# A hybrid attention/retention/MoE block: expert weights in 2 MB blocks of 16 KB runs, keys padded with zeros to 128 rows, second expert product 512 columns wide

## The chip, the cores and the metric

The kernel runs on one core of one Trainium2 chip. The metric is the device time of one execution in microseconds (us), taken as the median of several runs. A profile of one execution shows where that time goes. All times here are those of the kernel before the change.

## The reference, cut to what matters

The input is 512 tokens of width 1024, everything in float32.

```
xn   = rms_norm(h)
proj = xn @ w_in                      # 9728 columns: attention q/k/v, retention q/k/v/gate, branch gates
A: for each of 3 groups of 8 heads (head width 64): rotary on q and k, then
   scores = q . k / 8 in a window (groups 1 and 2: tokens strided by 4), masked softmax, times v
B: retention in both directions, chunks of 128, group norm, swish gate
h  = h + (sig(gA) * (A @ W_A) + sig(gB) * (B @ W_B)) @ w_out
hn = rms_norm(h)
router: top-1 of 8 expert groups, top-2 of 8 experts inside it (64 experts in all)
expert(x) = (silu(x @ w1[e]) * (x @ w3[e])) @ w2[e]     # w1, w3: 1024 x 512, w2: 512 x 1024
h  = h + weighted sum of the two experts of each token; final rms_norm
```

The weights of the 64 experts are 3 x 64 x 1024 x 512 x 4 bytes = 402.65 MB, and every one of them is read once.

## The kernel before, in words

There are two parts. In the first, the token-wise mixer, TensorE does long runs of products with `w_in`, the branch weights and `w_out`. Each weight tile and each activation is split into a high and a low half (`wH`, `wL`, `xH`, `xL`), and three products of 512 columns (L267 to L269 or L273 to L275) make one float32 product. A projection (`project`) of 512 columns has 8 x 4 x 3 such products. The program's order on each engine comes from a scheduler; it lays the products of one projection between the small products of the attention that came before.

Attention: `rotary_to` copies a projection to `qT` or `kT` (heads lie in pairs: block b holds head 2b on partitions 0 to 63 and head 2b+1 on partitions 64 to 127), exchanges halves by DMA into `sw`, multiplies on VectorE (L314) and GpSimd (L315) and adds on GpSimd (L316). The scores of a head are a product with 64 rows of `qT` against 64 rows of `kT`: L595 in `windows` (group 0, 192 keys per head, for two of the four token blocks in two parts of 64 queries), L639 (groups 1 and 2, 128 keys per head). A float32 product is two instructions on TensorE. VectorE masks them and finds the maximum (L551), ScalarE does the exponential (L553), TensorE transposes (L557), and the products with v follow (L604, L607, L648). There are 4 token blocks x 8 heads for each group.

In the second part, the experts go in 16 groups of 4. For a group, the tokens are gathered by products with a one-hot matrix (L769) into `xT` (32 slots per expert), then 16 blocks of `w13` (L973) and 8 blocks of `w2` (L1026, each 128 output columns of the four experts) are used. Between them stand the silu and the product of the halves (L993, L994), four transposes (L997) and copies (L999, L1000). The result is split (L1009, L1010) and scattered back (L1017 to L1019). The four experts of a group sit in four 32-column strips of TensorE's array.

Every block is 1 MB, 128 partitions x 8 KB, loaded by one DMA from SyncE's queue (`load`, L936) in program order. `wtile` hands out the places: eleven in `wA`; then two halves of `big`, used once; then a ring of the eleven and five more, four that hold the halves of the merged activation until `w_out` has read them (`xH0`, `xL0`, `xH1`, `xL1`) and one (`wB`) that lies where the mixer's weight halves were. The eleven and `big` lie where the mixer's right-hand pools were, which close after the last branch product. The loads of the first two weight tiles of a projection and of `w_out` (`raw`, L103) go on the same SyncE queue.

The last group of experts takes its `w2` in pieces of 256, 256, 256, 128 and 128 columns, each split, scattered and squared at once (`finish`), then the final norm and the output follow.

Of the kernel before, what the change touches and what calls it, by code (L numbers as in the profile page):

```python
# [10 lines left out]
F32 = mybir.dt.float32  # L11
# [10 lines left out]
P = 128  # L22
# [15 lines left out]
NWA = 11  # L38
NK2 = 4
# [29 lines left out]
def hybrid_block(ctx, tc, a, out):  # L69
# [86 lines left out]
    class Halves:  # L156


        def __init__(self):
            self.t = []  # L160
            for i in range(2):
                t_ = xp.tile([P, 4, S], F32R, name=self.tag + "01"[i])
                self.t.append(t_)
# [7 lines left out]
    class Hi(Halves):  # L171
        tag = "xH"

    class Lo(Halves):
        tag = "xL"
# [11 lines left out]
    xH = Hi()  # L187
    xL = Lo()
# [106 lines left out]
    def rotary_to(dst, dilated):  # L295
# [4 lines left out]
        def evac(b, ps):  # L300
# [8 lines left out]
            for k in range(2):  # L309
# [6 lines left out]
                nc.gpsimd.tensor_tensor(d, d, w, op=ALU.add)  # L316
# [228 lines left out]
    rec0 = at.tile([P, NT, REC], F32, name="rec0")  # L545
    orders = (nat, dil4, dil4)
# [15 lines left out]
    def windows(qT, kT, v4):  # L562
# [14 lines left out]
        for t in range(NT):  # L577
# [9 lines left out]
            for slot, hh in enumerate((0, 1, 4, 5)):  # L587
                po = (hh % 2) * HD
                ps = tmp()
                sm = rp.tile([P, 512], F32, name="sd", bufs=6)  # L590
                for i in range(2):
                    cs = slice(i * W, (i + 1) * W)
                    blk = hh // 2 + i
                    for qs, k0 in parts_:
                        nc.tensor.matmul(ps[qs, cs], qT[po:po + HD, blk, t * P + qs.start:t * P + qs.stop],  # L595
                                         kT[po:po + HD, blk, k0:k0 + W], start=True, stop=True)
                    probs(rec, hh + 2 * i, ps[:, cs], sm[:, cs], masks[:, mo_:mo_ + W])
                prT = transposed_probs(ps, sm, 3)
                oc = slice(slot * (HD + 1), (slot + 1) * (HD + 1))
                for i in range(2):  # L600
                    full = slice(2 * i * P, (2 * i + 1) * P)
                    po = i * HD
                    for qs, k0 in parts_:
                        nc.tensor.matmul(po_ps[i][qs, oc], prT[:, full][:, qs],  # L604
                                         values(k0 + po, 0, P, hh + 2 * i), start=True, stop=False)
                    for qs, k0 in parts_:
                        nc.tensor.matmul(po_ps[i][qs, oc], prT[po:po + HD, P:2 * P][:, qs],  # L607
                                         values(k0 + (1 - i) * P, po, HD, hh + 2 * i), start=False, stop=True)
            for i in range(2):
                nc.scalar.copy(rec[:, :NH * (HD + 1)].rearrange("p (x z w) -> p x z w", x=2, z=2)[:, :, i],  # L610
                               po_ps[i][:, :4 * (HD + 1)].rearrange("p (x w) -> p x w", x=2))

    for g in range(3):
        qT, kT = qk_tiles()
        project_in(512 * g, None, rotary_to(qT, g > 0))
        project_in(1536 + 512 * g, None, rotary_to(kT, g > 0))
# [8 lines left out]
        if g == 0:  # L625
            windows(qT, kT, v4)
            continue
        for t in range(NT):
            rec_t = at.tile([P, REC], F32, name="rec", bufs=2)
            rec = rec_t[:, :]  # L630
            for h0 in range(0, NH, 4):
                ps = tmp()
                sm = rp.tile([P, 512], F32, name="sd", bufs=6)
                for i in range(4):
                    hh = h0 + i
                    po = (hh % 2) * HD
                    cs = slice(i * P, (i + 1) * P)
                    ts = slice(t * P, (t + 1) * P)
# [86 lines left out]
    yrH = Hi()  # L725
    yrL = Lo()
# [12 lines left out]
    mH = Hi()  # L739
    mL = Lo()  # L740
# [23 lines left out]
    wA = ctx.enter_context(tc.tile_pool(name="wA", bufs=NWA, side="right"))  # L764

# [148 lines left out]
    w2 = a["moe_w2c"]  # L914
    nw = [0]
    spare = [(xp, "xH0"), (xp, "xL0"), (xp, "xH1"), (xp, "xL1"), (mo, "wB")]
    big0 = big.tile([P, 2 * 2048], F32, name="big")
    res = [None]

    def wtile():  # L920
        i = nw[0]
        nw[0] += 1
        if NWA <= i < NWA + 2:
            return big0[:, (i - NWA) * 2048:(i - NWA + 1) * 2048]
        i = (i if i < NWA else i - 2) % (NWA + len(spare))
        if i < NWA:
            t_ = wA.tile([P, 2048], F32, name="wa")
        else:
            pool, tag = spare[i - NWA]
            t_ = pool.tile([P, 2048], F32, name=tag)  # L930
# [12 lines left out]
    def experts(g, ranks, cols=None, first=False):  # L943
# [7 lines left out]
        xT = mo.tile([P, NK, P], F32, name="xT", bufs=3)  # L951
# [37 lines left out]
        ohT = mo.tile([P, S], F32R, name="k2", bufs=NK2)  # L989
        nc.scalar.copy(ohT, ps)  # L990

        sl = mo.tile([P, FF], F32, name="k2", bufs=NK2)
# [5 lines left out]
        hdT = mo.tile([P, 4, P], F32, name="k2", bufs=NK2)  # L998
# [5 lines left out]
        yH = mo.tile([P, D], F32R, name="xT", bufs=3)  # L1004
        yL = mo.tile([P, D], F32R, name="xT", bufs=3)
# [159 lines left out]
```

## Time and profile before

| | |
|---|---|
| median of 3 runs (lowest, highest) | 1665.96 us (1661.69, 1669.53) |
| the profiled execution: time, span from first to last instruction | 1663.84 us, 1662.1 us |
| TensorE, VectorE, ScalarE, GpSimd busy | 83%, 34%, 20%, 11% of the span |
| mean granted TensorE clock | 0.913 of full speed |
| DMA | 476.56 MB, mean 287 GB/s |

Busy shares are means over parts with different limits, so they have to be read part by part: the profile cuts the span into 40 slices, and a stretch of it can be asked for by its start and end.

### The profile page before, as it was taken

The numbers are of one execution on the slowest core, as the hardware profiler recorded it, in microseconds if no ns is written. First come the engines' busy times: TensorE is split into PE (matmuls) and PEld (weight loads), VectorE is DVE, ScalarE is ACT, GpSimd is POOL, SyncE is SP. The second block draws the span as 40 slices with busy tenths as digits, with TensorE's granted clock in tenths as the row PEclk, the third lists the DMA queues.
The fourth block names the chain that finished last, engine by engine and source line by source line (L and its number), as shares of the span: only waits on it lengthen the run. The fifth ranks groups of instructions, "written<-read, shape, count | busy, mean of one in ns | idle before, by whom it ended". The sixth has DMA issues, their size and how long they took to land. (4 is left out here: it accounts for less than half of the span.)

```text
span 1662.1 us, 27242 instructions
## 1 busy us (share of the span) xinstructions
PE 1386.6 (83%) x11699; PEld 915.9 (55%) x11699; DVE 561.7 (34%) x1241; ACT 328.7 (20%) x618; POOL 182.4 (11%) x137
## 2 busy tenths in 40 slices
PE   7999999999999999988776776776776786687674
PEld 6878787686876778754442442342353354244243
DVE  7556463554634544442220120120221121022014
ACT  5332334334346333210000000000000000000002
POOL 2214260231502211000000000000000000000001
PEclk9999999999999999998987887897898788888787
DMA  6324343233323423989999999999999999999995
GB/s 179 111 77 105 91 137 90 77 102 96 96 90 90 141 76 107 398 341 421 421 421 422 422 422 422 422 421 422 422 421 421 422 422 422 421 422 421 422 421 213
DMA packets 98509, 476.56 MB, mean 287 GB/s; under 512 B 17296, under 2 KB 17808, under 8 KB 49168
## 3 DMA queue, kind: packets, MB, share of 16 engines
q1 hardware_dynamic: 97344, 474.76, 72.8%
q8 instruction: 94, 1.54, 0.4%
q14 instruction: 31, 0.25, 0.0%
q10 hardware_dynamic: 1040, 0.00, 0.0%
HBM read 459.96 MB, written 4.26 MB: 279 GB/s over the span
## 5 line engine op out<-in xcount | busy, mean ns | idle before, releaser
L973 PE MATMUL acc<-wa,xT 128*32 128x512 f32 x1408 | 212.4, 716 | 83.7 <-DMA wa<-in_moe_w_dram 83.7
L213 DVE SCALAR_TENSOR_TENSOR wL<-raw,nwx,wH 128x512 fp32r<-128x512 f32 x152 | 138.0, 937 | 106.8 <-ACT wH L212 106.6
L268 PE MATMUL acc<-xL,wH 128*128 128x512 f32 x416 | 172.0, 413 | 0.0
L267 PE MATMUL acc<-xH,wH 128*128 128x512 f32 x416 | 168.8, 406 | 1.2 <-ACT kT L667 1.2
L973 PEld LDWEIGHTS acc<-wa,xT 128*32 128x32 f32 x1408 | 37.7, 117 | 237.2 <-DMA wa<-in_moe_w_dram 176.2
L269 PE MATMUL acc<-xH,wL 128*128 128x512 f32 x416 | 168.0, 404 | 0.0
L1026 PE MATMUL acc<-wa,k 128*32 128x128 f32 x2816 | 113.9, 319 | 56.8 <-DMA wa<-in_moe_w2c_dram 52.4
L1026 PEld LDWEIGHTS acc<-wa,k 128*32 128x32 f32 x2816 | 89.0, 129 | 81.2 <-DMA wa<-in_moe_w2c_dram 65.0
L212 ACT ACTIVATE wH<-raw,nwx 128x512 fp32r<-128x512 f32 x152 | 103.1, 716 | 150.1 <-PE acc L275 55.8
L273 PE MATMUL acc<-wH,xH 128*128 128x512 f32 x320 | 127.6, 400 | 0.2 <-ACT rt L536 0.2
L274 PE MATMUL acc<-wL,xH 128*128 128x512 f32 x320 | 127.5, 398 | 0.1
L275 PE MATMUL acc<-wH,xL 128*128 128x512 f32 x320 | 127.4, 398 | 0.0
L994 DVE SCALAR_TENSOR_TENSOR k<-k,gsl,acc 128x512 f32<-128x512 f32 x16 | 12.0, 748 | 332.8 <-issue 283.2
L769 PE MATMUL tmp<-oh,h 128*128 128x128 f32 x960 | 110.6, 276 | 0.3 <-DVE big L1019 0.3
L769 PEld LDWEIGHTS tmp<-oh,h 128*128 128x128 f32 x960 | 108.7, 192 | 3.7 <-DVE big L1019 3.2
L152 POOL TENSOR_TENSOR rr<-rv,mhalf 128x1 f32<-128x1 f32 x8 | 4.9, 622 | 947.0 <-ACT jk L1061 935.9
L1010 DVE TENSOR_TENSOR xT<-acc,xT 128x512 fp32r<-128x512 f32 (+2 forms) x35 | 22.6, 646 | 231.9 <-ACT xT L1009 231.8
L267 PEld LDWEIGHTS acc<-xH,wH 128*128 128x128 f32 x416 | 78.4, 189 | 22.4 <-issue 2.5
L268 PEld LDWEIGHTS acc<-xL,wH 128*128 128x128 f32 x416 | 78.5, 189 | 21.5 <-issue 2.3
L269 PEld LDWEIGHTS acc<-xH,wL 128*128 128x128 f32 x416 | 78.5, 189 | 18.1 <-issue 1.5
L1019 DVE TENSOR_TENSOR big<-big,tmp 128x512 f32<-128x512 f32 (+2 forms) x132 | 76.6, 635 | 21.7 <-PE tmp L1018 21.7
L1017 PE MATMUL tmp<-xT,k 128*128 128x512 f32 (+2 forms) x140 | 61.5, 462 | 22.9 <-ACT xT L1009 22.1
(259 smaller groups left out, 1705.3 us busy)
## 6 DMA issues: line engine op xcount, KB each, us to landing
wa<-in_moe_w_dram SPq DMA_DIRECT2D x176, 1024.0 KB, 19.8
wa<-in_moe_w2c_dram SPq DMA_DIRECT2D x88, 1024.0 KB, 19.9
raw<-in_w_in_dram SPq DMA_DIRECT2D x76, 512.0 KB, 3.7
xH<-in_moe_w_dram SPq DMA_DIRECT2D x32, 1024.0 KB, 19.8
xL<-in_moe_w_dram SPq DMA_DIRECT2D x31, 1024.0 KB, 19.7
xL<-in_moe_w2c_dram SPq DMA_DIRECT2D x16, 1024.0 KB, 19.8
xH<-in_moe_w2c_dram SPq DMA_DIRECT2D x16, 1024.0 KB, 19.8
wB<-in_moe_w_dram SPq DMA_DIRECT2D x15, 1024.0 KB, 19.6
```

Of the source, the lines that this page charges most:

```text
L212: nc.scalar.activation(wH[:, k, :], raw[:, k, :], AF.Copy, scale=sc)
L213: nc.vector.scalar_tensor_tensor(wL[:, k, :], raw[:, k, :], sc, wH[:, k, :], op0=ALU.mult, op1=ALU.subtract)
L267: nc.tensor.matmul(ps[tt], wh[:, cs], srcH.blk(kt), **fl)
L268: nc.tensor.matmul(ps[tt], wh[:, cs], srcL.blk(kt), start=False, stop=False)
L269: nc.tensor.matmul(ps[tt], wl[:, cs], srcH.blk(kt), start=False, stop=(kt == nk - 1))
L273: nc.tensor.matmul(ps[tt], aH, wh, **fl)
L274: nc.tensor.matmul(ps[tt], aH, wl, start=False, stop=False)
L275: nc.tensor.matmul(ps[tt], aL, wh, start=False, stop=(kt == nk - 1))
L769: nc.tensor.matmul(gp[j // 4][:, (j % 4) * P:(j % 4 + 1) * P], h[:, t, j * P:(j + 1) * P], oh_t.rearrange("p e c -> p (e c)"), start=(t == ...
L973: nc.tensor.matmul(p_[e * CAP:(e + 1) * CAP, :], xT[:, j, e * CAP:(e + 1) * CAP], wt[:, e * FF:(e + 1) * FF], start=(j == 0), stop=(j == N ...
L1019: nc.vector.tensor_tensor(hs_[:, t, cs], (h if first else hs_)[:, t, cs], ps, op=ALU.add)
L1026: nc.tensor.matmul(py[e * CAP:(e + 1) * CAP, o:o + P], hdT[:, i, e * CAP:(e + 1) * CAP], w4[:, e, i, :], start=(i == 0), stop=(i == 3))
```

## The change

The blocks of expert weights become 2 MB, 128 partitions x 16 KB: one for each of the eight 128-row slices of `w13` holds w1 and w3 of the four experts; one for each of the four 128-row slices of `w2` holds all 1024 output columns. The high and low halves of an activation move into one tile of 16 KB a partition for each half of the width (`x0`, `x1`), so that each of them is one place for a block. The places are five `wA`, `big` and `wk` (each used once), `x0`, `x1` and two `wB`: eleven in all, of which nine form the ring. The work tiles of a group lie where `wk` was. The `w2` products of all but the last group write 512 columns and end both halves of the output at the last block. The last group keeps blocks of output columns, and its last block comes in two DMAs.

The keys are written by GpSimd into `kP`, with a copy for the even and one for the odd head of a block, in which the other head's 64 partitions are zero. One product over 128 rows then gives the scores of both heads of a block side by side: 384 columns in group 0, 256 in groups 1 and 2. The added sum becomes two adds of 64 partitions, and two memsets zero `kP` once. `kP` has one buffer where `kT` had two.

```diff
-NWA = 11
+NGRP = NE // EG
+NWA = 5
+NWB = 2
+SLOT = 4096
...
+    def hi_lo():
+        t = []
+        for i in range(2):
+            t_ = xp.tile([P, 2, 4, S], F32R, name=f"x{i}")
+            t.append(t_)
+        return [Part([t_[:, z] for t_ in t]) for z in range(2)]
...
-                nc.gpsimd.tensor_tensor(d, d, w, op=ALU.add)
+                if pad is None:
+                    nc.gpsimd.tensor_tensor(d, d, w, op=ALU.add)
+                else:
+                    for z in range(2):
+                        hp = slice(z * HD, (z + 1) * HD)
+                        nc.gpsimd.tensor_tensor(pad[hp, b - 1 + k, z, :], d[hp], w[hp], op=ALU.add)
...
+    kP = at.tile([P, 4, 2, S], F32, name="kP")
+    for z in range(2):
+        nc.gpsimd.memset(kP[(1 - z) * HD:(2 - z) * HD, :, z, :], 0.0)
...
-            for slot, hh in enumerate((0, 1, 4, 5)):
+            for slot in range(4):
...
+                for qs, k0 in parts_:
+                    nc.tensor.matmul(ps[qs, :2 * W], qT[:, slot, t * P + qs.start:t * P + qs.stop],
+                                     kP[:, slot, :, k0:k0 + W], start=True, stop=True)
                 for i in range(2):
-                    for qs, k0 in parts_:
-                        nc.tensor.matmul(ps[qs, cs], qT[po:po + HD, blk, t * P + qs.start:t * P + qs.stop],
-                                         kT[po:po + HD, blk, k0:k0 + W], start=True, stop=True)
-                    probs(rec, hh + 2 * i, ps[:, cs], sm[:, cs], masks[:, mo_:mo_ + W])
+                    probs(rec, hh + i, ps[:, cs], sm[:, cs], masks[:, mo_:mo_ + W])
...
+                for i in range(0, 4, 2):
+                    nc.tensor.matmul(ps[:, i * P:(i + 2) * P], qT[:, (h0 + i) // 2, ts], kP[:, (h0 + i) // 2, :, ts],
+                                     start=True, stop=True)
                 for i in range(4):
-                    nc.tensor.matmul(ps[:, cs], qT[po:po + HD, hh // 2, ts], kT[po:po + HD, hh // 2, ts],
-                                     start=True, stop=True)
-                    probs(rec, hh, ps[:, cs], sm[:, cs], masks[:, 3 * HD:3 * HD + P] if g == 1 else masks[:, 9 * HD:])
+                    probs(rec, h0 + i, ps[:, cs], sm[:, cs],
+                          masks[:, 3 * HD:3 * HD + P] if g == 1 else masks[:, 9 * HD:])
...
+    ring = [(wA, "wa")] * NWA + [(xp, "x0"), (xp, "x1")] + [(mo, "wB")] * NWB
+    once = [(big, "big"), (wk, "wk")]
+    slots = ring[:NWA] + once + ring[NWA:]
...
+        pool, tag = slots[i] if i < len(slots) else ring[(i - len(slots)) % len(ring)]
+        t_ = pool.tile([P, SLOT], F32, name=tag, bufs={"wa": NWA, "wB": NWB}.get(tag, 1))
...
         for j in range(NK):
+            wt = load(block(w13, g, j)).rearrange("p (w e f) -> p w e f", w=2, e=EG)
             for w_, p_ in enumerate((p1, p3)):
-                wt = load(block(w13, g, 2 * j + w_))
                 for e in range(EG):
                     nc.tensor.matmul(p_[e * CAP:(e + 1) * CAP, :], xT[:, j, e * CAP:(e + 1) * CAP],
-                                     wt[:, e * FF:(e + 1) * FF], start=(j == 0), stop=(j == NK - 1))
+                                     wt[:, w_, e, :], start=(j == 0), stop=(j == NK - 1))
...
         if cols is None:
+            py = [acc(), acc()]
+            for i in range(4):
+                wt = load(block(w2r, g, i)).rearrange("p (e d) -> p e d", e=EG)
+                for hf in range(2):
+                    for e in range(EG):
+                        nc.tensor.matmul(py[hf][e * CAP:(e + 1) * CAP, :], hdT[:, i, e * CAP:(e + 1) * CAP],
+                                         wt[:, e, hf * 512:(hf + 1) * 512], start=(i == 0), stop=(i == 3))
             css = [slice(0, 512), slice(512, D)]
-            for cs in css:
-                py = acc()
-                for b in range(4):
-                    columns(load(block(w2, g, cs.start // P + b)), py, b * P)
-                split(cs, py, nc.scalar)
+            for cs, p_ in zip(css, py):
+                split(cs, p_, nc.scalar)
             scatter(css)
...
-    nc = _bacc.Bacc("TRN2", target_bir_lowering=False, num_devices=1)
+    nc = _bacc.Bacc("TRN2", target_bir_lowering=False, num_devices=1, dynamic_dma_scratch_size=1024)
```

## Rows read from the trace of the kernel before

**Rows 1.** The page's second part, the span in 40 slices of 41.6 us: the busy share of TensorE in tenths, and what the DMA engines moved.

```profile
PE   7999999999999999988776776776776786687674
...
GB/s 179 111 77 105 91 137 90 77 102 96 96 90 90 141 76 107 398 341 421 421 421 422 422 422 422 422 421 422 422 421 421 422 422 422 421 422 421 422 421 213
```

**Rows 2.** Busy time by stretch. Columns: the stretch, its length, busy us of PE, PEld, DVE, ACT and POOL with their instructions in brackets, granted clock, busy share of the 16 DMA engines, GB/s.

```profile
200.00:300.00 100.00, 99.89 (x540) 75.11 (x538) 48.95 (x86) 38.67 (x69) 28.45 (x19) 1.00 0.40 111
500.00:600.00 100.00, 97.70 (x494) 75.06 (x492) 54.50 (x90) 48.03 (x76) 23.41 (x16) 1.00 0.36 107
...
600.00:661.50 61.50, 61.50 (x266) 49.55 (x265) 28.98 (x34) 15.22 (x19) 12.52 (x8) 1.00 0.28 94
...
722.50:1600.00 877.50, 648.52 (x7569) 350.10 (x7565) 153.39 (x322) 43.71 (x77) 0.00 (x0) 0.85 1.01 421
```

**Rows 3.** What SyncE's queue issued around the start of the weight stream, in order of time: start, length, line, tile, count.

```profile
661.50 0.82 SPq L936 DMA_DIRECT2D wa<-in_moe_w_dram  x2
...
692.99 0.33 SPq L936 DMA_DIRECT2D xH<-in_moe_w_dram  x1
709.20 0.33 SPq L936 DMA_DIRECT2D xH<-in_moe_w_dram  x1
...
710.10 0.38 SPq L936 DMA_DIRECT2D wB<-in_moe_w2c_dram  x1
720.19 4.62 SPq L936 DMA_DIRECT2D wa<-in_moe_w2c_dram  x6
```

**Rows 4.** TensorE's products in order of time in group 1 of the attention (start, length, line, tile, shape of the stationary and of the moving side, count): a pair for one head, and four transposes, among projection products.

```profile
363.89 0.40 PE L275 MATMUL acc<-wH,xL 128*128 128x512 f32 x1
364.21 0.48 PE L639 MATMUL tmp<-kT,qT 64*128 64x128 f32 x2
...
364.97 0.39 PE L268 MATMUL acc<-xL,wH 128*128 128x512 f32 x1
365.19 0.40 PE L269 MATMUL acc<-xH,wL 128*128 128x512 f32 x1
...
369.13 0.40 PE L269 MATMUL acc<-xH,wL 128*128 128x512 f32 x1
369.38 0.60 PE L557 MATMUL tmp<-ident,sd 128*128 128x128 f32 x4
...
370.05 0.39 PE L268 MATMUL acc<-xL,wH 128*128 128x512 f32 x1
```

**Rows 5.** The same in group 0: a pair for one head of 192 keys.

```profile
253.92 0.39 PE L275 MATMUL acc<-wH,xL 128*128 128x512 f32 x1
254.24 0.59 PE L595 MATMUL tmp<-kT,qT 64*128 64x192 f32 x2
...
255.10 0.40 PE L268 MATMUL acc<-xL,wH 128*128 128x512 f32 x1
```

**Rows 6.** The costliest groups of instructions, the row of the scores of groups 1 and 2 (line, engine, operation, tiles, shapes, count, busy us, mean ns of one, idle before it), and the DMA issues, the row of the `wA` blocks of `w13` (count, KB each, median us from issue to landing).

```profile
L639 PE MATMUL tmp<-kT,qT 64*128 64x128 f32 x128 | 31.1, 323 | 0.2 <-DVE rec L551 0.2
...
wa<-in_moe_w_dram SPq DMA_DIRECT2D x176, 1024.0 KB, 19.8
```

**Rows 7.** GpSimd's last adds to the keys of groups 0 and 1 in order of time.

```profile
244.63 3.44 POOL L316 TENSOR_TENSOR kT<-kT,sw 128x512 f32<-128x512 f32 x2
...
356.87 3.44 POOL L316 TENSOR_TENSOR kT<-kT,sw 128x512 f32<-128x512 f32 x2
```

**Rows 8.** DMA by stretch of 2 us in the two gaps of the stream. Columns: the stretch, its length, granted clock, busy share, GB/s.

```profile
704.00:706.00 2.00, 1.00 0.76 320
706.00:708.00 2.00, 1.00 0.16 66
708.00:710.00 2.00, 1.00 0.00 0
710.00:712.00 2.00, 1.00 0.81 246
718.00:720.00 2.00, 1.00 0.15 61
720.00:722.00 2.00, 1.00 0.40 74
722.00:724.00 2.00, 1.00 0.88 356
```

**Rows 9.** The same columns: a stretch at the start, in which the input comes in runs of 4 KB and some weights in runs of 2 KB, and the middle of the stream in runs of 8 KB.

```profile
7.00:11.00 4.00, 1.00 1.04 417
...
800.00:1600.00 800.00, 0.85 1.01 422
```

**Rows 10.** The same columns at the end of the stream.

```profile
1628.00:1630.00 2.00, 0.50 1.04 438
1630.00:1632.00 2.00, 1.00 0.65 266
...
1640.00:1642.00 2.00, 1.00 0.43 180
```

**Rows 11.** TensorE in order of time: from the last scatter of one group over the gather (left out between) to its next weight product, and the last w13 block of the last group.

```profile
1106.86 0.39 PE L1018 MATMUL tmp<-xT,k 128*128 128x512 f32 x1
1114.46 4.50 PE L973 MATMUL acc<-wa,xT 128*32 128x512 f32 x40
...
1623.36 1.93 PE L973 MATMUL acc<-wa,xT 128*32 128x512 f32 x8 [1.44 <-DMA wa<-in_moe_w_dram]
```

More of the change, by code (lines that the diff above doesn't have):

```diff
@@ L153, in rsqrt_begin, with __init__ @@
         return v, r
[L156 to L163, printed above, removed]
+    class Part:
+        def __init__(self, t):
+            self.t = t
         def blk(self, k):
@@ L764, in hybrid_block @@
     wA = ctx.enter_context(tc.tile_pool(name="wA", bufs=NWA, side="right"))
+    early = ExitStack()
+    wk = early.enter_context(tc.tile_pool(name="wk", bufs=1, side="right"))
     def gather(t, oh_t, gp, js=range(NK)):
@@ L913, in hybrid_block @@
     w13 = a["moe_w13"]
-    w2 = a["moe_w2c"]
+    w2r = a["moe_w2r"]
+    w2c = a["moe_w2c"]
     nw = [0]
-    spare = [(xp, "xH0"), (xp, "xL0"), (xp, "xH1"), (xp, "xL1"), (mo, "wB")]
-    big0 = big.tile([P, 2 * 2048], F32, name="big")
+    ring = [(wA, "wa")] * NWA + [(xp, "x0"), (xp, "x1")] + [(mo, "wB")] * NWB
+    once = [(big, "big"), (wk, "wk")]
+    slots = ring[:NWA] + once + ring[NWA:]
+    work = []
     res = [None]
@@ L941, in block, with experts @@
         return w[bass.ds(g, 1), i:i + 1].rearrange("g i p n -> p (g i n)")
-    def experts(g, ranks, cols=None, first=False):
+    def experts(g, ranks, cols=None, first=False, ends=False):
         es = bass.ds(g * EG, EG)
@@ L969, in experts @@
         for j in range(NK):
+            wt = load(block(w13, g, j)).rearrange("p (w e f) -> p w e f", w=2, e=EG)
             for w_, p_ in enumerate((p1, p3)):
-                wt = load(block(w13, g, 2 * j + w_))
                 for e in range(EG):
                     nc.tensor.matmul(p_[e * CAP:(e + 1) * CAP, :], xT[:, j, e * CAP:(e + 1) * CAP],
-                                     wt[:, e * FF:(e + 1) * FF], start=(j == 0), stop=(j == NK - 1))
+                                     wt[:, w_, e, :], start=(j == 0), stop=(j == NK - 1))
+        if not work:
+            early.close()
+            wk2 = ctx.enter_context(tc.tile_pool(name="wk2", bufs=1, side="right"))
+            w_ = wk2.tile([P, 2 * D + S], F32R, name="yp")
+            work.append(w_)
+            w_ = wk2.tile([P, 2 * FF], F32, name="hid")
+            work.append(w_)
+        yH = work[0][:, :D]
+        yL = work[0][:, D:2 * D]
+        ohT = work[0][:, 2 * D:]
+        sl = work[1][:, :FF]
+        hdT = work[1][:, FF:].rearrange("p (i s) -> p i s", i=4)
         grl = mo.tile([P, NT, EG, 2], F32, name="grl", bufs=2)
@@ L1029, in experts @@
         if cols is None:
-            css = [slice(0, 512), slice(512, D)]
-            for cs in css:
-                py = acc()
-                for b in range(4):
-                    columns(load(block(w2, g, cs.start // P + b)), py, b * P)
-                split(cs, py, nc.scalar)
+            py = [acc(), acc()]
[5 more added lines that the diff above has]
+                                         wt[:, e, hf * 512:(hf + 1) * 512], start=(i == 0), stop=(i == 3))
+            css = [slice(0, 512), slice(512, D)]
+            for cs, p_ in zip(css, py):
+                split(cs, p_, nc.scalar)
             scatter(css)
         else:
-            wts = [load(block(w2, g, b)) for b in range(NK)]
-            tail.enter_context(tc.manual_schedule(engines=all_engines))
+            wts = []
+            for b in range(NK // 2):
+                t_ = wtile()
+                src = w2c[b:b + 1].rearrange("b p n -> p (b n)")
+                for c in range(0, SLOT, SLOT // 2 if b == NK // 2 - 1 else SLOT):
+                    n = SLOT // 2 if b == NK // 2 - 1 else SLOT
+                    nc.sync.dma_start(out=t_[:, c:c + n], in_=src[:, c:c + n])
+                wts += [t_[:, :SLOT // 2], t_[:, SLOT // 2:]]
+            if ends:
+                tail.enter_context(tc.manual_schedule(engines=all_engines))
             for c0, n in cols:
@@ L1047, in experts @@
                 scatter([cs])
-                finish(c0, n)
+                if ends:
+                    finish(c0, n)
     last = [(0, 256), (256, 256), (512, 256), (768, 128), (896, 128)]
@@ L1059, in finish @@
         for t in range(NT):
-            junk = mo.tile([P, 256], F32, name="jk", bufs=2)
+            junk = mo.tile([P, 256], BF16, name="jk", bufs=2)
             nc.scalar.activation(junk[:, :n], res[0][:, t, c0:c0 + n], AF.Square, accum_out=parts[t][:, i:i + 1])
     tail = ExitStack()
-    NGRP = NE // EG
     for g in range(NGRP):
-        experts(g, ranks, cols=last if g == NGRP - 1 else None, first=g == 0)
+        experts(g, ranks, cols=last if g == NGRP - 1 else None, first=g == 0, ends=g == NGRP - 1)
         if g == 2:
@@ L1119, in hybrid_block @@
             nc.vector.tensor_scalar(ranks, ranks, float(CAP), None, op0=ALU.add)
-            with tc.For_i(0, NGRP, 1) as g:
+            with tc.For_i(0, NGRP - 1, 1) as g:
                 experts(g, ranks)
+            experts(NGRP - 1, ranks, cols=last)
         for c0, n in last:
```

70 lines of the change are left out of this document (24 added, 46 removed).

## Prediction

> **What bounds the kernel now.** I read the slices first, then busy time by stretch, then the queue that issues the weights, then TensorE in order of time. The slices fall into two halves with different limits [rows 1]: up to about slice 16 TensorE is busy nearly all the time while DMA moves about 100 GB/s; from there to the end TensorE drops to six to eight tenths and DMA stands at 421 to 422 GB/s. By stretch it is sharper: TensorE is busy 99.9 of 100 us from 200 to 300 and all 61.5 us before 661.5, with VectorE at half; in the stream DMA is busy for the whole time (share 1.01) and TensorE 74% [rows 2]. So the time is the sum of a TensorE part that ends at 661.5, where the first weight block is issued [rows 3], a DMA part, and a tail. In the first part a microsecond counts if it is TensorE's; in the second only if it is the stream's. A weight lands 19.8 us after its issue [rows 6]; at 422 GB/s a block of 1.049 MB takes 2.49 us, so eight blocks are always under way.
>
> **The padded keys.** Projection products (L268 to L269) start 0.23 us apart [rows 4]. From L275 to L268 with one head's pair and one projection product between them takes 1.08 us where 0.46 would do, so a pair costs 0.62 us, of which its 0.48 us row shows only a part. There are 128 instructions [rows 6], 64 pairs: 64 x 0.62 = 39.7 us. No row shows a 256-column float32 product over 128 rows. The nearest is the four transposes: 4 x 128 columns over all 128 rows cost 0.92 - 0.46 = 0.46 us [rows 4]. A padded product has two passes of 256 columns, as many columns, so I take 0.46 us for each of the 32: 14.7 us. Saved 25.0 us. The streaming work is the same in both; what goes is the change of shape between 64 and 128 rows, some 0.39 us a pair (0.62 less half of 0.46). If that cost stayed with each padded product, the saving would be 39.7 - 32 x 0.85 = 12.5 us; that is the lower bound, and 25 is nearly the upper one.
>
> Group 0: a pair of 192 columns costs 1.18 - 0.46 = 0.72 us where it stands alone [rows 5], two heads 1.44; the padded product has 768 column passes, 1.5 x 0.46 = 0.69 us. But many heads there follow other 64-row products (L607, unchanged) and share the change of shape with them, which L607 then pays alone. I take 0.2 us for each of 16 products, 3 us, with -3 and 12 (16 x 0.75) as bounds. TensorE part: 28 us. VectorE and ScalarE have the same instructions as before and half their time free [rows 2].
>
> What it adds on GpSimd: four adds per group more, at 3.44 / 2 = 1.7 us if half the partitions save nothing, 6.9 us. In group 0 the last add ended at 248.1 and the first scores started at 254.2; in group 1 at 360.3 and 364.2 [rows 4, 5, 7]. Now it would be 255.0 and 367.2, but the late blocks are those of the heads 4 to 7, whose turn comes several microseconds after the first. I cost it at nothing; if the first scores wait for the last add, it is 0.8 + 3.0 + 3.0 = 7 us at most, less what projection products can fill. The single `kP` holds back the next group's adds until the last scores are done; in between lies a projection of 96 x 0.23 = 22 us. Nothing there.
>
> **The start of the stream.** Before, 13 blocks have places at once, two more at 693.0, three more at 709.2 to 710.1, and the first reused place at 720.2 [rows 3]. DMA ran dry twice [rows 8]: the stretches 704 to 712 miss 102 + 356 + 422 + 176 GB/s, times 2 us over 422 is 5.0 us; 718 to 724 miss 361 + 348 + 66, 3.7 us. After, there are seven early places of 2 MB and `x0` at the same point as the two at 693.0: 16 MB by 709 instead of 15, so the first gap shrinks by 2.5 us. Then `x1` and two `wB` give 6.3 MB, 14.9 us of stream, enough to reach 725, while the first reused place comes free about 1.3 us later than before (both products of a slice). The second gap goes. Together 6 us; 2.5 and 8.7 are the bounds.
>
> **The stream's rate.** 402.65 MB at 422 GB/s are 954 us, so 1% is 9.5 us. What a run costs beside its bytes I take from two stretches [rows 9]. Counting what the engines were busy: 8 KB runs 1.01 x 16 x 8192 / 422 = 314 ns, runs of mostly 4 KB 1.04 x 16 x 4096 / 417 = 163 ns, so a run has a fixed part of 2 x 163 - 314 = 12 to 13 ns; 16 KB runs would take 615 ns, 431 GB/s. Counting the rates alone it is 2 x 157.2 - 310.6 = 4 ns, 424.5 GB/s. The short stretch is noisy and mixed, so I take the middle, 428 GB/s: 940.8 us, 13 us less. Bounds: nothing, and 20 us.
>
> [...]
>
> **The end.** The last 12 us of the stream run at half the rate and half the busy share [rows 10]: a part of the engines is done while the others finish. More bytes under way could let them drift further apart; I take no change, and 6 us more as a bound. The last block of `w13` now brings w1 and w3 together, so one more 1 MB's worth of products stands after its landing: 1.9 us at the low clock [rows 11], part of it beside the silu. I add 1.5 us.
>
> **Sum.** 1663.84 (the profiled execution) - 28 - 6 - 13 + 1.5 = 1618.3; it lies 2.1 us under the median of the runs, so the median becomes 1620 us. The 512-column `w2` products and fewer instructions change nothing here, since TensorE waits for DMA in the stream.
>
> **Rivals.**
> - *The rate stays at 422.* For it: the two rates are within 1.2% though one stretch has half the run length. Against: the busy share is higher there. 1620 + 13 = 1633.
> - *The change of shape stays with the padded product* (12.5 us saved instead of 25, nothing in group 0). For it: no row shows the padded shape. Against: the transposes, over all rows, lie between the same projection products and cost only their columns. 1620 + 15.5 = 1636, with the old rate 1649.
> - *Padding throws away array.* Two heads of 64 rows in different halves of the array could stream side by side; padded, each pair streams twice the time. If heads ran so before, the change would lose the saved streaming, 32 x 0.23 = 7 us, instead of winning 28: 1655, within 0.5% with the old rate (1668). Against it: between two heads lie three projection products, so no two stream together [rows 4]. [...]
> - *Slower: the coarse ring runs dry at each group.* Nine places of 2 MB, each given back only when all of it is used, and both halves of `w2` end at the last block. TensorE leaves weights untouched from 1106.9 to 1114.5 [rows 11] and some microseconds more around the four transposes. DMA stops only if it stays away for more than about eight blocks, 8 x 4.97 = 40 us; against that stand some 12. To undo the 46 us won, each of 15 boundaries must cost 3.1 us; at 4 us it is 1620 + 60 = 1680.
>
> **How the numbers follow.** Forecast 0.5, old rate 0.25, change of shape stays 0.13, array thrown away 0.05, ring dry 0.07. 0.5% of the time, 8.3 us, is about what a measurement of this kernel tells from no change: from 1658 to 1674. Faster: the first three, 0.88; same: the fourth and little else, 0.05; slower: 0.07. The range runs from the forecast with the upper rate, the upper group 0 and the larger gap (1620 - 7 - 6 - 2.7) to the change of shape at the old rate, 1604 to 1650.
>
> **What would show it.** The first weight issue near 633 instead of 661.5; 32 products of 256 columns in groups 1 and 2 with about 0.46 us between their neighbours; no stretch without DMA after the first gap of some 2.5 us; GB/s of 428 in the slices of the stream, with weight packets halved. A first issue at 645 or later, a stream at 422, or zeros in the GB/s row at a period of a group would each make a term wrong.

## The result, and the profile after

| | before | after |
|---|---|---|
| median (lowest, highest; 4 runs each, side by side) | 1664.66 us (1661.69, 1669.53) | 1621.41 us (1621.28, 1624.02) |
| profiled execution: time, span | 1663.84 us, 1662.1 us | 1621.28 us, 1619.6 us |
| TensorE busy, mean granted clock | 83%, 0.913 | 83%, 0.927 |
| DMA packets, bytes | 98,509, 476.56 MB | 70,980, 476.14 MB |

The ratio is 0.9741, with a 95% interval of 0.9715 to 0.9767. The predicted 1620 us holds to 1.4 us, but this closeness is luck, since two errors cancel in it: between the two profiled executions the TensorE part gave 20.5 us and not 28, and the DMA part 22.0 and not 17.5.

The page after, TensorE and GB/s in 40 slices of 40.5 us; [rows 1] answers to it:

```profile
PE   7999999999999999997775785776776676677674
...
GB/s 183 104 88 108 92 140 96 53 117 93 118 112 133 149 79 132 349 405 428 428 427 429 428 428 428 428 427 429 428 428 428 429 427 429 428 427 428 428 427 224
```

The shape is the same, with 427 to 429 where 421 and 422 stood. No slice of the stream falls below until the last, so the ring of places does not run dry at the groups.

SyncE's issues around the start of the stream after (start, length, tile, count); [rows 3] answers to it:

```profile
524.49 0.33 SPq L942 DMA_DIRECT2D wk<-in_moe_w_dram  x1
...
640.76 0.34 SPq L942 DMA_DIRECT2D wa<-in_moe_w_dram  x1
...
672.50 0.33 SPq L942 DMA_DIRECT2D x<-in_moe_w_dram  x1
688.72 0.33 SPq L942 DMA_DIRECT2D x<-in_moe_w2r_dram  x1
...
700.32 0.33 SPq L942 DMA_DIRECT2D wa<-in_moe_w2r_dram  x1
```

The first `wA` block goes out at 640.76 (661.50 before) and `x1`, the place that opens when `w_out` is done, at 688.72 (709.20): 20.5 us earlier. This issue of `x1` is the best mark to cut the time at, since what lies before it is TensorE's and what lies after it the stream's. From it to the end of the span are 952.9 us before (1662.1 - 709.2) and 930.9 after, 22.0 less.

The first row is one that the prediction did not see coming: the block for `wk` goes out 116 us before the others, because the attention's keys and records (`kP`, `rec`), in whose memory `wk` lies, are done with by then: the wait of SyncE's queue ends with L707 on VectorE, which reads the last `rec`.

The DMA by stretch after (stretch, length, clock, share, GB/s): first gap, middle, and end of the stream; [rows 8 to 10] answer to it:

```profile
680.00:682.00 2.00, 1.00 0.62 254
682.00:684.00 2.00, 1.00 0.06 25
684.00:686.00 2.00, 1.00 0.01 4
686.00:688.00 2.00, 1.00 0.00 0
688.00:690.00 2.00, 1.00 0.60 115
690.00:692.00 2.00, 1.00 0.64 229
800.00:1500.00 700.00, 0.87 1.01 428
...
1590.00:1592.00 2.00, 1.00 0.90 365
1592.00:1594.00 2.00, 1.00 0.58 246
...
1596.00:1598.00 2.00, 1.00 0.50 209
1598.00:1600.00 2.00, 1.00 0.28 102
```

There is one gap, of 9 us (what is missing to 428 GB/s from 680 to 692), and none after. The half-rate end lasts some 8 us, from 1591 to 1599, where it lasted 12 [rows 10].

TensorE in order of time in group 1 after; [rows 4] answers to it:

```profile
362.50 0.40 PE L275 MATMUL acc<-wH,x 128*128 128x512 f32 x1
362.74 1.02 PE L645 MATMUL tmp<-kP,qT 128*128 128x256 f32 x4
363.41 0.58 PE L267 MATMUL acc<-x,wH 128*128 128x512 f32 x1
363.83 0.40 PE L268 MATMUL acc<-x,wH 128*128 128x512 f32 x1
```

From L275 to L268 it is 1.33 us where 0.46 would do without scores: 0.87 us for two padded products (four heads), 0.43 each. The prediction said 0.46. Behind the products with v (L657), where most of them stand, they cost the same: from L269 at 371.71 to L268 at 373.85 it is 2.14 us, of which 0.46 go to the two projection products and 0.81 to the L657, as much as these add at 488.95, where no scores follow. That leaves 0.87 us again.

### The profile page after: what moved, and what is told of

The parts are those of the page before. It is cut to its first block, busy times and chain, and to the rows that moved or that the text cites. A ratio compares the mean times of both kernels' runs of the same rounds, so it can differ in the third digit from the quotient of the medians.

```text
span 1619.6 us, 20935 instructions
## 1 busy us (share of the span) xinstructions
PE 1338.7 (83%) x8707; PEld 825.7 (51%) x8707; DVE 562.0 (35%) x1241; ACT 317.8 (20%) x614; POOL 208.4 (13%) x151
## 2 busy tenths in 40 slices
DMA packets 70980, 476.14 MB, mean 294 GB/s; under 512 B 14240, under 2 KB 14752, under 8 KB 46112
## 4 chain that ended last, share of the span: by engine, by line
PE 55%; DMA 38%; DVE 4%; ACT 1%; issue 1%; POOL 1%; SPq 0%; DVEq 0%; ACTq 0%; POOLq 0%
DMA wa<-in_moe_w2r_dram 23%; DMA x<-in_moe_w2r_dram 10%; PE acc L267 6%; PE acc L268 6%; PE acc L269 6%; PE tmp L778 6%; PE acc L979 5%; PE acc L274 4%; PE acc L273 4%; PE acc L275 4%; DMA wa<-in_moe_w_dram 2%; DMA wB<-in_moe_w2c_dram 2%; PE tmp L1031 2%; PE acc L1049 2%; PE tmp L1032 2%; PE tmp L645 1%
## 5 line engine op out<-in xcount | busy, mean ns | idle before, releaser
L979 PE MATMUL acc<-wa,xT 128*32 128x512 f32 x1120 | 156.6, 693 | 69.5 <-DMA wa<-in_moe_w_dram 69.5
L267 PE MATMUL acc<-x,wH 128*128 128x512 f32 x416 | 170.1, 409 | 3.1 <-ACT kT L676 3.1
L269 PE MATMUL acc<-x,wL 128*128 128x512 f32 x416 | 167.8, 403 | 0.0
L268 PE MATMUL acc<-x,wH 128*128 128x512 f32 x416 | 167.8, 403 | 0.0
L1049 PE MATMUL acc<-wa,hid 128*32 128x512 f32 x560 | 88.8, 764 | 54.4 <-DMA wa<-in_moe_w2r_dram 50.2
L274 PE MATMUL acc<-wL,x 128*128 128x512 f32 x320 | 127.8, 399 | 0.1
L273 PE MATMUL acc<-wH,x 128*128 128x512 f32 x320 | 127.4, 399 | 0.1
L275 PE MATMUL acc<-wH,x 128*128 128x512 f32 x320 | 127.4, 398 | 0.0
L979 PEld LDWEIGHTS acc<-wa,xT 128*32 128x32 f32 x1120 | 34.2, 119 | 171.4 <-DMA wa<-in_moe_w_dram 93.7
L267 PEld LDWEIGHTS acc<-x,wH 128*128 128x128 f32 x416 | 79.1, 190 | 23.5 <-ACT kT L676 3.5
L268 PEld LDWEIGHTS acc<-x,wH 128*128 128x128 f32 x416 | 78.8, 189 | 18.9 <-issue 1.4
L269 PEld LDWEIGHTS acc<-x,wL 128*128 128x128 f32 x416 | 78.8, 189 | 18.0 <-issue 0.2
L979 PE MATMUL acc<-wB,xT 128*32 128x512 f32 x480 | 64.0, 662 | 28.7 <-DMA wB<-in_moe_w_dram 28.7
L979 PE MATMUL acc<-x,xT 128*32 128x512 f32 x416 | 58.8, 702 | 30.0 <-DMA x<-in_moe_w_dram 30.0
```

The costliest lines, as they stand in the source:

```text
L267: nc.tensor.matmul(ps[tt], wh[:, cs], srcH.blk(kt), **fl)
L268: nc.tensor.matmul(ps[tt], wh[:, cs], srcL.blk(kt), start=False, stop=False)
L269: nc.tensor.matmul(ps[tt], wl[:, cs], srcH.blk(kt), start=False, stop=(kt == nk - 1))
L273: nc.tensor.matmul(ps[tt], aH, wh, **fl)
L274: nc.tensor.matmul(ps[tt], aH, wl, start=False, stop=False)
L275: nc.tensor.matmul(ps[tt], aL, wh, start=False, stop=(kt == nk - 1))
```

## The experiments

Every ratio is to runs of the kernel before on the same chip, where it took 1663 to 1665 us. The medians of the experiments are also set beside the 1621.41 us of the kernel after, which come from other runs, so a microsecond or two between them tells nothing. The x1 mark is used throughout. One execution of each kernel was profiled, and the part ahead of x1 differs by some microseconds between kernels that do the same there: the issue of the exchange of group 0's keys lies between 228.8 and 231.5, the mark itself, with padded keys, between 686.0 and 693.9. The part after x1 repeats: 930.7 to 931.1 us in six kernels that load the weights as after does.

**Each half of the change alone.** First the padded keys on the blocks of before:

```diff
+    kP = at.tile([P, 4, 2, S], F32, name="kP")
...
+                    nc.tensor.matmul(ps[:, i * P:(i + 2) * P], qT[:, (h0 + i) // 2, ts], kP[:, (h0 + i) // 2, :, ts],
```

> The kernel before with the padded keys alone (blocks, places and w2 products as before). What the trace after suggests: the TensorE part ends 20.5 us earlier, as the places x0 and x1 did, so the first weight issue is near 641 and the time 1644 us (1642 to 1647); group 0 saves nothing, groups 1 and 2 about 19.5. The step on record, 28 us: first issue near 633, 1637 us. Were the change of shape to stay with the padded product (12.5 us): 1652 us.

Then the blocks, places and `w2` products of after with the keys of before:

```diff
-        project_in(1536 + 512 * g, None, rotary_to(kT, g > 0, kP))
+        project_in(1536 + 512 * g, None, rotary_to(kT, g > 0))
...
+                    nc.tensor.matmul(ps[:, cs], qT[po:po + HD, hh // 2, ts], kT[po:po + HD, hh // 2, ts],
+                                     start=True, stop=True)
```

> The kernel after with the keys of before (unpadded, two buffers); blocks of 2 MB, places and 512-column w2 products as after. If the two halves of the change add up, 1665 - 22 = 1643 us (1640 to 1645): 13 from the rate (428 GB/s), some 6 from the start of the stream, the rest at the end of the stream; first weight issue near 661. If the blocks only gain because TensorE is done earlier, or the two share a gain, more than 1648.

Measured: keys alone 1645.94 us, ratio 0.9883 [0.9863, 0.9903] (one of its four executions took 3164.99 us and was not followed up; the median counts all four, the ratio the other three, 1644.97 to 1646.39); blocks alone 1641.38 us, 0.986 [0.9842, 0.9878]. Against 1664.4 that is 18.5 and 23.0 us, 41.5 together, where both at once gave 43.3. The x1 mark splits them cleanly: 691.00 with the keys alone, 709.92 with the blocks alone, and from there to the end 952.8 us with the keys alone and 930.8 with the blocks alone. The keys work only before the mark, the blocks only behind it. The 28 us that the prediction had for the TensorE part would have made 1637 us; they are refuted. By either median or mark, with the old blocks or the new, the keys are worth 18 to 21 us. Both kernels also carry the smaller `dynamic_dma_scratch_size` of the change, which was not tried alone; with the keys alone it changes nothing behind the mark.

**What sets the rate.** After changed two things at once, the bytes of a DMA and the length of a run. Five kernels take them apart. Two DMAs of half the columns (1 MB, 8 KB runs):

```diff
-        nc.sync.dma_start(out=t_, in_=src)
+        for c in range(0, SLOT, SLOT // 2):
+            nc.sync.dma_start(out=t_[:, c:c + SLOT // 2], in_=src[:, c:c + SLOT // 2])
```

> The kernel after, each 2 MB block loaded by two DMAs of one half of its columns: 1 MB each, runs of 8 KB; places and products unchanged. Theory that the run length sets the rate: 422 GB/s in the middle of the stream, 400.5 MB take 949 instead of 936 us, so 1634 us (up to 1638 if the long half-rate end of before comes back as well). Rival, that the rate comes from the larger places or fewer products: 428 GB/s and 1621 us.

One DMA of 2 MB from a block that lies in DRAM as two halves (2 MB, 8 KB runs):

```diff
-        nc.sync.dma_start(out=t_, in_=src)
+        nc.sync.dma_start(out=t_.rearrange("p (w n) -> p w n", w=2), in_=src)
...
-    return {"moe_w13": np.ascontiguousarray(w13).reshape(NGRP, NK, P, SLOT),
...
+    return {"moe_w13": np.ascontiguousarray(w13).reshape(NGRP, NK, 2, P, SLOT // 2),
```

> The kernel after, one DMA of 2 MB for each block as after, but the block lies in DRAM as two halves, so that each partition is filled by two runs of 8 KB. Run-length theory: 422 GB/s in the middle of the stream and 1635 us, as with two DMAs of 8 KB runs. Rival, that it is the size of a DMA (2 MB, half as many issues): 428 GB/s and 1621 us.

Four DMAs of a quarter of the columns (512 KB, 4 KB runs; the same loop with `SLOT // 4`):

> The kernel after, each 2 MB block loaded by four DMAs of a quarter of its columns: 512 KB each, runs of 4 KB. With the fixed part that 422 GB/s at 8 KB and 428 at 16 KB give (310.6 x 2 - 612.5 = 9 ns a run), a 4 KB run takes 160 ns: 410 GB/s, 400.5 MB in 976 instead of 936 us, 1661 us. If the row of before at 416 to 417 GB/s for runs of mostly 4 KB is the rate: 961 us, 1646 us. If the run length does not set the rate: 1621 us.

Two DMAs of 64 partitions (1 MB, 16 KB runs), first the lower and the upper 64:

```diff
-        nc.sync.dma_start(out=t_, in_=src)
+        for p0 in range(0, P, HD):
+            nc.sync.dma_start(out=t_[p0:p0 + HD], in_=src[p0:p0 + HD])
```

> The kernel after, each 2 MB block loaded by two DMAs of 64 partitions each: 1 MB each as in the other split, but runs of 16 KB as after. Run-length theory: 428 GB/s and 1621 us (1619 to 1624). Rival, that the bytes of one DMA or the bytes under way set the rate: 422 GB/s and 1634 us. If 64 partitions leave some engines without work, well below 422 GB/s and over 1640 us.

then the even and the odd ones:

```diff
-        nc.sync.dma_start(out=t_, in_=src)
+        for p0 in range(2):
+            nc.sync.dma_start(out=t_[p0::2], in_=src[p0::2])
```

> The kernel after, each 2 MB block loaded by two DMAs of 1 MB in runs of 16 KB: one for the even partitions, one for the odd ones. The split into the lower and the upper 64 partitions ran at 217 GB/s with all engines busy. If it is the neighbourhood of the 64 partitions that halves it, and the run length that sets the rate otherwise: 428 GB/s and 1621 us. If any DMA into 64 partitions is slow: about 217 GB/s, over 2100 us. If the 1 MB of a DMA sets the rate: 422 GB/s, 1635 us.

The middle of the stream in each (stretch, length, granted clock, share, GB/s). Two DMAs of 8 KB runs:

```profile
800.00:1500.00 700.00, 0.89 1.01 422
```

One DMA of 2 MB in 8 KB runs:

```profile
800.00:1500.00 700.00, 0.87 1.01 422
```

4 KB runs:

```profile
800.00:1500.00 700.00, 1.00 1.03 412
```

Even and odd partitions, 16 KB runs:

```profile
800.00:1500.00 700.00, 0.87 1.01 428
```

| DMA, run | GB/s | median | from x1 to the end |
|---|---|---|---|
| 2 MB, 16 KB (after) | 428 | 1621.41 us | 930.9 us |
| 1 MB, 16 KB (even, odd) | 428 | 1626.27 us | 933.1 us |
| 2 MB, 8 KB | 422 | 1634.10 us | 942.6 us |
| 1 MB, 8 KB | 422 | 1635.66 us | 943.4 us |
| 512 KB, 4 KB | 412 | 1656.09 us | 965.1 us |

At 16 and at 8 KB the rate follows the run and not the DMA: 1 and 2 MB give the same. At 4 KB run and DMA were shortened together, so that step is not taken apart. Over the 16 engines of the profile a run costs 16 x 16384 / 428 = 612.5 ns, 16 x 8192 / 422 = 310.6 ns and 16 x 4096 / 412 = 159.1 ns: by estimate, twice the shorter less the longer leaves a fixed part of 7 to 9 ns, about the same in both steps. The row at 417 GB/s of the start [rows 9], in runs of mostly 4 KB, was too high for this. The 8 KB kernels also divide the 22.0 us behind the mark: on the new places they take 942.6 and 943.4 us, so 11.7 to 12.5 us go with the run, and the other 9.5 to 10.3 with the places, the start and the end.

The even-odd kernel's 1626 is not the rate: of the 4.9 us over after 2.2 stand behind the mark, which came at 693.90; the rest lies ahead of it and stays open. The lower-upper split did not answer its question, but it gave one of its own. Its four executions took 2146 to 2267 us, with a median of 2246.76; the longest was profiled, and this is the page's GB/s row:

```profile
GB/s 158 91 97 112 121 66 98 127 104 150 84 184 214 214 216 218 216 218 219 220 222 224 224 233 243 266 304 298 310 331 317 342 362 318 231 215 220 237 238 148
```

For the first 600 us of the stream 214 to 224 is half of 428, and the share of the engines stands at 1.01 (217 GB/s from 800 to 1000). From 1300 to 1900 us the rate rises, up to 362 in a slice (311 from 1500 to 1700), and falls back behind it, with the share at 1.01 as before; why was not tried. The engines are called busy although they move half as much: the share is 1.01 at 217 GB/s and 1.01 at 428, so it says that they have work, not that they move all they could. The even and the odd partitions, 64 to a DMA as well, ran at 428, and the split into lower and upper halves itself at up to 362 in a slice, so DMAs of 64 partitions are not held to half the rate. What held this kernel there for its first 600 us no run shows.

**Change of shape or cost of a product.** After, but with two products of 128 columns over 128 rows for a block:

```diff
-                for i in range(0, 4, 2):
-                    nc.tensor.matmul(ps[:, i * P:(i + 2) * P], qT[:, (h0 + i) // 2, ts], kP[:, (h0 + i) // 2, :, ts],
-                                     start=True, stop=True)
+                for i in range(4):
+                    nc.tensor.matmul(ps[:, i * P:(i + 1) * P], qT[:, (h0 + i) // 2, ts],
+                                     kP[:, (h0 + i) // 2, i % 2, ts], start=True, stop=True)
```

> The kernel after, but in groups 1 and 2 the padded keys of a block are used in two products of 128 columns over 128 rows instead of one of 256: as many columns, twice the instructions, no product over 64 rows. Theory that what the pair cost before was the change between 64 and 128 rows: two products cost what one did (0.43 us), so at most 1 us more, 1621 to 1623 us. Rival, that it was a fixed cost of each product (0.39 us): 32 x 0.39 = 12.5 us more, 1634 us.

TensorE in order of time, the same place as above:

```profile
363.36 0.40 PE L275 MATMUL acc<-wH,x 128*128 128x512 f32 x1
363.59 1.05 PE L645 MATMUL tmp<-kP,qT 128*128 128x128 f32 x8
364.40 0.48 PE L267 MATMUL acc<-x,wH 128*128 128x512 f32 x1
364.72 0.39 PE L268 MATMUL acc<-x,wH 128*128 128x512 f32 x1
```

Eight instructions instead of four, and from L275 to L268 1.36 us instead of 1.33. The median is 1620.88 us. So here the columns set the cost, and not a fixed price for each product: twice as many of them for the same columns added 0.03 us for two blocks. That it is not the interruption of the projection either, the four transposes show where, in the kernel after, they stand one by one:

```profile
364.77 0.39 PE L269 MATMUL acc<-x,wL 128*128 128x512 f32 x1
365.10 0.33 PE L567 MATMUL tmp<-ident,sd 128*128 128x128 f32 x1
...
366.20 0.28 PE L567 MATMUL tmp<-ident,sd 128*128 128x128 f32 x1
...
366.55 0.39 PE L268 MATMUL acc<-x,wH 128*128 128x512 f32 x1
```

These 1.78 us hold five steps of 0.23 and the four transposes, which add 0.6 us where four in a row add 0.44: 0.04 us for each interruption by a product of the same shape. What is left for the 0.4 us that each pair lost before (0.62 less half of the 0.43 of a padded product) is the change between 64 and 128 rows and back, which the padding avoids. Why it costs that much no trace shows.

**Group 0.** After, but group 0 keeps its unpadded products:

```diff
-        project_in(1536 + 512 * g, None, rotary_to(kT, g > 0, kP))
+        project_in(1536 + 512 * g, None, rotary_to(kT, g > 0, kP if g else None))
...
-            windows(qT, v4)
+            windows(qT, kT, v4)
```

> The kernel after, but group 0 keeps the unpadded products (64 rows, 192 columns, heads 0 1 4 5 first); groups 1 and 2 padded. Trace after: group 0 saved nothing, so 1621 us (1619 to 1623). The step on record, 3 us saved there: 1624 us. If the padded form costs time in group 0 (its two-part products no longer stream side by side): 1618 us.

1622.33 us (1621.09 to 1628.63): no difference that can be told. From the exchange of group 0's keys to that of group 1 are 110.3 us, against 109.0 padded and 109.4 in the kernel before. Over all kernels this stretch takes 109.0 to 109.4 us padded and 109.4 to 110.4 unpadded, so padding group 0 is worth between nothing and 1.4 us. The trace says why it is so little. The two token blocks in two parts, before (scores of two heads, behind four products with v):

```profile
289.36 0.34 PE L604 MATMUL tmp<-v,sd 128*64 128x65 f32 x4
289.63 0.27 PE L607 MATMUL tmp<-v,sd 64*64 64x65 f32 x2
289.65 0.38 PE L595 MATMUL tmp<-kT,qT 64*64 64x192 f32 x2
289.73 0.23 PE L607 MATMUL tmp<-v,sd 64*64 64x65 f32 x2
289.79 0.49 PE L595 MATMUL tmp<-kT,qT 64*64 64x192 f32 x6
290.21 0.50 PE L269 MATMUL acc<-xH,wL 128*128 128x512 f32 x1
```

and after (scores of four heads):

```profile
276.74 0.33 PE L616 MATMUL tmp<-v,sd 64*64 64x65 f32 x4
277.00 1.51 PE L602 MATMUL tmp<-kP,qT 128*64 128x384 f32 x8
278.44 0.50 PE L267 MATMUL acc<-x,wH 128*128 128x512 f32 x1
```

Before, four L607 take 0.26 us by themselves (276.74 to 277.00), so the eight L595 of two heads cost 0.58 - 0.26 = 0.32 us. At the padded products' 0.43 us for 512 columns, their 8 x 192 columns would by estimate take 1.29 us one after another; the measured 0.32 us is a quarter of that, as if four of these 64x64 products ran at a time, and in the rows the first L595 starts 0.02 us behind an L607. After, two padded products cost 1.44 us, 0.72 for two heads. Eight times 0.40 us, 3.2 us, are lost in these two blocks, and the group as a whole did not lose, so about as much must come back in the other two. This is the rival of the array that padding throws away, in the one place where it holds. It points to a version better than both: pad only the blocks in one part, and let the others read 64 rows from the filled half of `kP`:

```diff
+                if one:
+                    nc.tensor.matmul(ps[:, :2 * W], qT[:, slot, t * P:(t + 1) * P],
+                                     kP[:, slot, :, parts_[0][1]:parts_[0][1] + W], start=True, stop=True)
...
+                    for qs, k0 in [] if one else parts_:
+                        nc.tensor.matmul(ps[qs, cs], qT[hp, hh // 2 + i, t * P + qs.start:t * P + qs.stop],
+                                         kP[hp, hh // 2 + i, z, k0:k0 + W], start=True, stop=True)
```

> The kernel after, but in group 0 only the two token blocks with one part keep the padded product; the two blocks in two parts use 64-row products again, read from the filled half of the padded keys. Theory from the traces: a two-part padded product costs 0.72 us, two heads of it in the unpadded form 0.32 (four 64x64 tiles share the array), so 8 x 0.40 = 3 us less in group 0 (from the exchange of its keys to that of group 1 106 us instead of 109.0), and about 1618 us against 1621 after. Rival, that the unpadded form only looked cheap because it stood beside other 64-row products: 109 us and 1621.

SyncE's exchanges of the keys of groups 0 and 1 in this version:

```profile
231.52 5.60 SPq L309 DMA_DIRECT2D sw<-kT  x8
...
337.84 5.60 SPq L309 DMA_DIRECT2D sw<-kT  x8
```

106.3 us, as expected, against 109.0 to 109.4 in all kernels with group 0 padded throughout, and 109.4 to 110.4 in those without padding there: the two blocks in one part win 3.0 to 4.1 us. The median is 1618.49 us (five executions, 1616.76 to 1619.20), ratio 0.9726 [0.9713, 0.974], some 3 us under after. The two ratios' intervals overlap, so the medians alone do not prove the step; the 2.7 us in the trace carry it.

**The first gap and the early place.** After without the place `wk`:

```diff
-    once = [(big, "big"), (wk, "wk")]
+    once = [(big, "big")]
```

> The kernel after without the place wk: six places instead of seven before x0, ten in all. Theory: what counts is the bytes that have places before x1 comes free (688.7), 2 MB fewer now, so 2.10 MB / 428 GB/s = 4.9 us more: 1626 us, with the first gap as long as after (9 us). Rival, that the stream would have waited anyway in its first gap: 1621 us.

and with `wk` held back until the last merged activation is written:

```diff
+        if nw[0] == NWA + 2:
+            nc.gpsimd.tensor_copy(t_[:, :1], mL.blk(7)[:, :1])
         nc.sync.dma_start(out=t_, in_=src)
```

> The kernel after, but the load into wk is held back until the last merged activation is written (near 640) instead of being issued at 524.5. Theory: what counts is how many places are full by the time x1 comes free (688.7), not when they were filled, so the same time (1620 to 1623 us), with the first gap in the stream shrunk from 9.1 to about 4.2 us. Rival, that 2 MB read early are 4.9 us saved: 1626 us.

Without it: 1628.84 us (1627.47 to 1630.81), 7.4 more than after where 4.9 were expected. From x1 to the end it is 935.6 us, 4.7 more, as the bytes say; the rest lies ahead of the mark (693.5), in the part that differs from kernel to kernel, and stays open. Held back: 1621.79 us, and its gap (the same columns):

```profile
684.00:686.00 2.00, 1.00 0.68 291
686.00:688.00 2.00, 1.00 0.04 16
688.00:690.00 2.00, 1.00 0.87 188
```

These three rows miss (137 + 412 + 240) GB/s, times 2 us over 428 is 3.7 us, where after has 9. The total is the same, and so is the time from x1 to the end (930.8). So the length of this gap says nothing by itself: the DMA has filled every place that there is and waits for `x1`. What counts is how many bytes have found a place by then.

## Why the prediction was right, and where not

**TensorE part, predicted 28 us, measured 20.5.** Between fixed marks of the queue, before and after: to the exchange of group 0's keys 229.8 and 228.8 (nothing changed there, 1.0 us of variation), on to that of group 1 109.4 and 109.0, on to that of group 2 97.2 and 85.4, on to the loads of the retention's branch weights 136.0 and 128.4, on to x1 136.8 and 137.2. The padded groups 1 and 2 gave 11.9 + 7.6 = 19.5 us instead of 25. The first of these repeats: the stretch takes 85.3 to 85.6 us in every kernel with padded keys, 97.2 and 97.3 in the two without. The second does not: 125.5 to 130.7 padded, 136.0 and 139.1 unpadded, so that its 7.6 could as well be some microseconds more or less. The mechanism and the price of the new product were right (0.43 for 0.46). What failed is "64 x 0.62": 0.61 us is the price of a pair alone between projection products. Of the 64, 14 came right behind L648, whose products have the shape 128*64. TensorE in order of time at one of them, in the kernel before:

```profile
370.52 0.40 PE L267 MATMUL acc<-xH,wH 128*128 128x512 f32 x1
370.85 0.69 PE L648 MATMUL tmp<-v,sd 128*64 128x65 f32 x16
371.46 0.49 PE L639 MATMUL tmp<-kT,qT 64*128 64x128 f32 x2
371.88 0.50 PE L268 MATMUL acc<-xL,wH 128*128 128x512 f32 x1
372.21 0.40 PE L269 MATMUL acc<-xH,wL 128*128 128x512 f32 x1
```

From L267 to L269 it is 1.69 us, 1.22 more than these two projection products need. Where L648 stands without scores, it adds 0.81:

```profile
526.09 0.40 PE L268 MATMUL acc<-xL,wH 128*128 128x512 f32 x1
526.41 0.69 PE L648 MATMUL tmp<-v,sd 128*64 128x65 f32 x16
...
527.37 0.39 PE L267 MATMUL acc<-xH,wH 128*128 128x512 f32 x1
```

So this pair cost 0.40. That makes 50 x 0.61 + 14 x 0.40 = 36 us for 39.7, less 32 x 0.43 = 14: 22 us, 11 for each group. Group 0 was costed with this sharing in mind, groups 1 and 2 were not. The stretch that repeats bears the 11 out (11.9). What is missing to 22 lies in the other one, where a wait of L267 on ScalarE is 3.1 us (at L676) for 1.2 before (at L667); the four transposes of a slice, which now mostly lie in two pieces between projection products, take some 0.52 us instead of 0.44. The rest of that stretch's spread stays open.

**Group 0, 3 us.** Measured 0.4, and 0 to 1.4 over all kernels. The bounds (-3 and 12) held. What the term left out are the 64x64 products that ran side by side in two of the four token blocks (eight in 0.32 us, by estimate 1.29 one after another).

**GpSimd's adds, nothing.** Right: no L645 and no L602 waited for GpSimd in the trace. The adds do end later (the last one of group 0 at 253.2 and of group 1 at 365.2, behind the first scores at 252.7 and 362.7), but the late ones belong to the late heads.

**Start of the stream, 6 us.** Right in sum. The second gap, 3.7 us, is gone. The first did not shrink from 5 us to 2.5 but grew to 9, since `wk` had been read long before; its 2 MB are missing from the bytes after x1 all the same. By x1, 16.8 MB have their places instead of 15.7, which is 2.5 us of stream. So the gap of 2.5 us that the prediction named as a sign was the wrong sign of a right term.

**Rate, 13 us.** Right: 428 GB/s, and 386.9 MB after x1 / 422 less the same / 428 is 12.9 us. The packets of 8 KB and more fell by half, from 49,341 to 24,868. The fixed part lies between the two estimates (4 and 12 to 13 ns); that the middle of the two came out was luck, since nothing in the trace before could tell between them. A stream of 4 KB runs alone then went at 412 GB/s, not at the 417 of the trace before, which was a short and mixed stretch.

**End, 1.5 us more.** From the start of the products with the last `w13` block to the start of the last scatter's last product are 23.85 us instead of 23.22, so 0.6. What was costed at nothing came out as a gain: the half-rate end is 4 us shorter, about 2 us of stream. What sets this length stays open: it is 12 us in the kernel before and with the keys alone, 6 to 9 in all kernels with the new blocks, whether in runs of 4, 8 or 16 KB. The terms come to 12.9 + 3.7 + 2.5 + 2 - 0.6 = 20.5 of the 22.0 us; the rates are rounded to 1 GB/s, worth 2 us, so the difference can't be told.

**Rivals.** Old rate and ring that runs dry: refuted by the 428 in every slice. Change of shape that stays: refuted by 0.43 us. Thrown-away array: wrong for the sum, true in half of group 0. The prediction looked for heads that run together in group 1 alone; the trace before has them in group 0, at 289.79 above. That the 512-column `w2` products change nothing was not tried alone. In the stream TensorE goes on waiting for weights, as the group of L979 shows (count, busy, mean, idle before it):

```profile
L979 PE MATMUL acc<-wa,xT 128*32 128x512 f32 x1120 | 156.6, 693 | 69.5 <-DMA wa<-in_moe_w_dram 69.5
```

## What to carry to other kernels

Price an instruction by where it stands, not by one clean example: a pair over 64 rows cost 0.61 us alone among products over 128, 0.40 right behind products of the shape 128*64, and eight 64x64 products of 192 columns took 0.32 us, a quarter of what the estimate gives for one after another. Where the stream is the bound, look at the length of the runs first: 4, 8 and 16 KB gave 412, 422 and 428 GB/s, and at 8 and 16 KB the size of the DMA made no difference. And cut the time at a mark that separates two bounds: here the two halves of the change then add up to a tenth of a microsecond behind it.

## What the runs showed of the hardware that was not expected

DMAs into the lower and the upper 64 partitions in turn ran at 214 to 224 GB/s for 600 us, with the engines' share at 1.01; into the even and the odd partitions they ran at 428. And the granted clock of TensorE in the middle of the stream (800 to 1500) was 1.00 with 4 KB runs in four DMAs a block; in the kernels that streamed at 421 to 428 GB/s it lies between 0.83 and 0.89. TensorE was busy 641 of the 700 us with the 4 KB runs, against 489 to 553. The cause was not tried, and the stream was the bound in each.
